# The last row block's normalisation: its middle 256 columns scaled by ScalarE and offset by GpSimd, and its factor computed ahead of most centring

## The chip, the cores and the metric

The kernel runs on one core of a Trainium2 chip. The metric is the time of one execution on the device in microseconds (us). A core has TensorE (matrix products, PE in the profile), VectorE (DVE), ScalarE (ACT), GpSimd (POOL) and SyncE (SP, which here only issues DMAs), each with an instruction queue that it works off in order. They share an on-chip memory, SBUF; TensorE writes its results to a second one, PSUM.

## The reference

One decoder layer over 512 tokens of width 1024: two attention branches, an output projection, a layer norm, then a gated MLP with a causal convolution, and a second layer norm. All of it is float32. What matters here is the very last step, the second layer norm:

```python
ffn_out = (silu(h_gate) * h_val) @ w_down
x = layer_norm(alpha * x + (1 + gt2) * ffn_out, ln2_g, ln2_b)

def layer_norm(x, g, b):
    mu = mean(x, axis=-1); var = mean((x - mu) ** 2, axis=-1)
    return (x - mu) * rsqrt(var + 1e-5) * g + b
```

Mean and variance are taken along the 1024 columns of each row, so a row's normalisation can start only when its last column has been summed.

## The kernel before, in words

The 512 rows are handled as four blocks of 128 rows (the 128 partitions of SBUF); a block's 1024 columns lie in two tiles of 512, `r[i][0]` and `r[i][1]`. Every float32 product is done as three products of split operands. The down projection is a Strassen-like scheme of sums of quarter blocks; blocks 0 and 1 are finished and stored earlier, and the end of the kernel belongs to blocks 2 and 3.

In the last loop (L1345 to L1358), `i` is 0 for block 2 and 1 for block 3. TensorE computes the last products of that block's second half. For block 2 that is one piece of 512 columns; for block 3 there are two pieces of 256 columns, so that VectorE can work on the first while TensorE still computes the second. The first piece's product is added to the residual in SBUF (L1356). For the second piece TensorE adds the residual itself (L1350, with the identity and the split residual `rest`), so its sum stays in PSUM. For each piece `V.bn_stats` (L1357) gathers the row statistics; those of the first 512 columns have been gathered earlier (L1329).

`ln_stats` (L899) turns the statistics into the mean `mu` and the normalising factor `rs`: VectorE merges them (L901), ScalarE takes a square root (L903), VectorE adds epsilon to the variance (L904), takes the reciprocal of the root (L905) and refines it by a Newton step (L906, L907). All of these work on one column. The factor comes out as -2 times the wanted one; the row of gains `lnr[0]` was multiplied by -0.5 beforehand to make up for it.

`tail` (L1239) then finishes a block on VectorE, piece by piece: centring (L1245) computes (x - mu) * gain, and scaling (L1249) computes x * rs + offset, with the offset row `lnr[1]`. Both are one instruction with three operands, two of them tiles. After each scaling, SyncE issues the store of that piece (L1250). For block 3 the pieces are columns 0 to 511, 512 to 767 (the middle one) and 768 to 1023 (read from PSUM).

Order: SyncE's queue is kept in program order. On the other engines a scheduler orders instructions by program order as priority and by when it holds their operands to be ready; so it puts the centrings between the steps of `ln_stats`. `tc.issue_after(ins)` adds an edge that keeps the block's instructions behind `ins` on the same engine, with no wait of its own.

Of the kernel before, what the change touches and what calls it, by code (L numbers as in the profile page):

```python
# [11 lines left out]
AF = mybir.ActivationFunctionType  # L12
ALU = mybir.AluOpType
# [38 lines left out]
def layer_kernel(ctx: ExitStack, tc: tile.TileContext, out, xT, x, c8, wa0, wa1, bcol, w1, wct, wv, bf,  # L52
# [3 lines left out]
    V, S, G, PE = nc.vector, nc.scalar, nc.gpsimd, nc.tensor  # L56
# [14 lines left out]
    cnt, state = [0], {"load": 0, "proc": 0}  # L71

    def nm(s):
        cnt[0] += 1
        return f"{s}_{cnt[0]}"

    def bank():
        return pp.tile([P, 512], F32, name=nm("ps"), tag="ps")
# [41 lines left out]
    s = V.tensor_tensor(sel, s3, ident[:, 64:72], ALU.add)  # L120
    def top_half(ap):
        return ap.bitcast(BF16).rearrange("p (c t) -> p c t", t=2)[:, :, 1]

    ctop = top_half(crow)
    with tc.issue_after(s.ins):
        s = V.tensor_tensor(crow[32:40], c8s, top_half(c8s), ALU.subtract)
# [21 lines left out]
    def z(dt, s, shape=(P, 512)):  # L148
        return zp.tile(list(shape), dt, name=nm(s), tag="z", bufs=NZ)
# [748 lines left out]

    def ln_stats(st):  # L899
        mv = cons.tile([P, 8], F32, name=nm("mv"), tag="mv", bufs=2)  # L900
        V.bn_aggr(mv[:, 0:2], st)  # L901
        v, s, y, t = mv[:, 2:3], mv[:, 3:4], mv[:, 4:5], mv[:, 5:6]
        S.activation(s, mv[:, 1:2], AF.Sqrt, bias=epsc)  # L903
        V.tensor_scalar_add(v, mv[:, 1:2], EPS)  # L904
        V.reciprocal(y, s)  # L905
        V.scalar_tensor_tensor(t, y, y, v, ALU.mult, ALU.mult)  # L906
        V.scalar_tensor_tensor(y, t, -3.0, y, ALU.add, ALU.mult)  # L907
        return mv[:, 0:1], y

    def ln_row(n):  # L910
# [14 lines left out]
    lnr = []  # L925
# [17 lines left out]
    def o_norm(i):  # L943
        xn, ps2 = o_st.pop(i)
        st = cons.tile([P, 2, 6], F32, name=nm("st"), tag="st", bufs=2)
        for e in range(2):
            ps = ps2[e]
            V.scalar_tensor_tensor(xn[e], xn[e], ALPHA, ps, ALU.mult, ALU.add)
            V.bn_stats(st[:, e, :], xn[e])
        mu, rs = ln_stats(st)  # L950
        for e in range(2):
            V.tensor_scalar(xn[e], xn[e], mu, rs, ALU.subtract, ALU.mult)
        x1.append(xn)
# [83 lines left out]
    for n in range(2 * FT):  # L1037
# [7 lines left out]
        if n in (23, 27):  # L1045
            t = t13[(23, 27).index(n)][:, 0:512]
# [124 lines left out]
    for n in range(2 * FT):  # L1171
        if n < NSPLIT:
            h, l = items[wui[n]][4]
            ps = bks[n]
            up_mm(ps, h, l, slice(256, 512))
        else:
            ps = bank()
# [21 lines left out]
        t = z(F32, "cv")  # L1199
# [6 lines left out]
        if n % 2 == 1:  # L1206
            g, v = hc
# [31 lines left out]
    def tail(i, st, pieces, eng, src):  # L1239
        tb = slice(i * P, (i + 1) * P)  # L1240
        mu, rs = ln_stats(st[:, 0 : len(pieces), :])
        for (e, c0, c1), ps in zip(pieces, src):
            c = slice(e * 512 + c0, e * 512 + c1)
            v = r[i][e][:, c0:c1]
            V.scalar_tensor_tensor(v, v if ps is None else ps, mu, lnr[0][:, c], ALU.subtract, ALU.mult)  # L1245
        for e, c0, c1 in pieces:
            c = slice(e * 512 + c0, e * 512 + c1)
            v = r[i][e][:, c0:c1]
            V.scalar_tensor_tensor(v, v, rs, lnr[1][:, c], ALU.mult, ALU.add)  # L1249
            eng.dma_start(out[tb, c], v)  # L1250

    p1, u2, q1, u3, tm = [[fine(n) for _ in range(2)] for n in ("p1", "u2", "q1", "u3", "tm")]
# [45 lines left out]
    def first_rows(i):  # L1298
        st = stat_tile()
        for e in range(2):  # L1300
            V.bn_stats(st[:, e, :], r[i][e])
        tb = slice(i * P, (i + 1) * P)
        mu, rs = ln_stats(st[:, 0:2, :])
        for e in range(2):
            c, v = slice(e * 512, (e + 1) * 512), r[i][e]
            V.scalar_tensor_tensor(v, v, mu, lnr[0][:, c], ALU.subtract, ALU.mult)
            S.activation(v, v, AF.Copy, scale=rs)
            G.dma_start(out[tb, c], v, accum_op=ALU.add)
# [8 lines left out]
    lnr = lnr2  # L1317
# [13 lines left out]
    for n, k in enumerate(wi):  # L1331
        w = weights(k)
        for a, p in enumerate(range(2 * n, min(FP - LATE, 2 * n + 2))):
            t = ops[p][3]
# [4 lines left out]
    s = V.tensor_tensor(r[3][1], r[3][1], W1[1], ALU.add)  # L1339
# [5 lines left out]
    for i in range(2):  # L1345
        pieces = [(1, 0, 512)] if i == 0 else [(1, 0, 256), (1, 256, 512)]
        for n, (e, c0, c1) in enumerate(pieces):
            ps = bank()[:, 0 : c1 - c0] if i else W1[0]
            for m in range(2 * n):
                PE.matmul(ps, idr, rest[:, m * 256 : m * 256 + 256], start=m == 0, stop=False)  # L1350
            for q in range(LATE):
                t = ops[FP - LATE + q][3]
                product(ps, t[:, top[i]], t[:, bot[i]], wc[q][0][:, c0:c1], wc[q][1][:, c0:c1], i == 1 and n == 0 and q == 0, q == LATE - 1, i == 0)
            v = r[2 + i][e][:, c0:c1]
            if n == 0:
                V.tensor_tensor(v, v, ps, ALU.add)  # L1356
            V.bn_stats(sts[i][:, n + 1, :], ps if n else v)  # L1357
        tail(2 + i, sts[i], [(0, 0, 512)] + pieces, nc.sync, [None, None, ps] if i else [None] * 2)  # L1358
# [69 lines left out]
```

## Time and profile before

| | |
|---|---|
| median of 3 runs | 735.04 us (734.61 to 735.48) |
| the profiled execution | 734.07 us, its span 732.3 us |
| TensorE's granted clock | 0.997 |
| busy over the span: TensorE / VectorE / ScalarE / GpSimd | 722.5 / 601.1 / 391.7 / 88.0 us |

The profile's times count from the start of the span. Its lines name engine, source line, operation, output and inputs, shapes (partitions x elements) and types. A line with x2 or x3 merges neighbouring instructions; its duration runs from the first start to the last end. In square brackets stands how long the engine had been idle before, and what released it. In the rows of stages, after the length, come the busy time of TensorE, its weight loads, VectorE, ScalarE and GpSimd with the number of instructions, then the granted clock, the DMA engines' busy share and GB/s. In the groups of instructions the figures after the bar are the total busy time, the mean in ns, and the idle time ahead.

### The profile page before, as it was taken

Reading aid. Unit: us, or ns where it says so; the run is one execution under the profiler, and the core shown is the slowest. Engines: PE = TensorE matmul, PEld = TensorE weight load, DVE = VectorE, ACT = ScalarE, POOL = GpSimd, SP = SyncE. Lnnn points to the kernel's source line nnn. Section 1 sums busy time; section 2 is a strip of 40 time slices with the busy share of each in tenths; the row PEclk is TensorE's granted clock in tenths of the full one; section 3 lists DMA queues with packets and bytes.
Section 4 is the critical chain, followed back from the end, with each engine's and each line's share of the span. In section 5 each row is a group of like instructions: output and inputs, shape, how many; then the busy total and the mean of one; then the engine's idle time right before and its main releaser. Section 6 shows DMA issues by size and latency. Waiting matters only on the chain.

```text
span 732.3 us, 9843 instructions
## 1 busy us (share of the span) xinstructions
PE 722.5 (99%) x3444; PEld 602.5 (82%) x3444; DVE 601.1 (82%) x1041; ACT 391.7 (53%) x684; POOL 88.0 (12%) x142
## 2 busy tenths in 40 slices
PE   8999999999999999999999999999999999999995
PEld 5878888888888888888889888888888888888885
DVE  7978799778898886883687999978887887679996
ACT  5576466686885754442056553454453544347550
POOL 1045224352010000000000001000011010000010
PEclk9999999999999999999999999999999999999998
DMA  9953435323332241632075688587698777657734
GB/s 358 404 207 126 173 116 197 148 88 115 118 116 99 75 171 59 224 128 86 1 259 139 216 248 238 169 252 227 189 359 245 217 238 209 200 164 224 219 91 93
DMA packets 45202, 131.96 MB, mean 180 GB/s; under 512 B 6136, under 2 KB 6656, under 8 KB 45152
## 3 DMA queue, kind: packets, MB, share of 16 engines
q1 hardware_dynamic: 37888, 112.61, 44.6%
q0 software_dynamic: 4224, 10.30, 7.4%
q10 hardware_dynamic: 3040, 8.42, 3.1%
q8 instruction: 27, 0.44, 0.2%
q14 instruction: 23, 0.19, 0.1%
HBM read 118.39 MB, written 12.85 MB: 179 GB/s over the span
## 4 chain that ended last, share of the span: by engine, by line
PE 97%; DVE 1%; DMA 0%; ACT 0%; issue 0%; DVEq 0%
PE ps L152 19%; PE ps L154 19%; PE ps L153 19%; PE ps L1148 5%; PE ps L1149 5%; PE ps L1150 5%; PE ps L369 5%; PE ps L613 3%; PE ps L595 2%; PE ps L521 2%; PE ps L523 2%; PE ps L522 2%; PE ps L939 2%; PE ps L941 2%; PE ps L940 2%; PE ps L547 1%
## 5 line engine op out<-in xcount | busy, mean ns | idle before, releaser
L217 ACT ACTIVATE wh<-raw 128x1024 fp32r<-128x1024 f32 (+1 forms) x105 | 109.0, 1040 | 106.5 <-PE ps L153 43.2
L94 DVE TENSOR_TENSOR wl<-raw,wh 128x1024 fp32r<-128x1024 f32 (+2 forms) x114 | 137.3, 1205 | 32.4 <-ACT wh L217 31.6
L152 PE MATMUL ps<-u2h,wh 128*128 128x512 f32 (+1 forms) x376 | 141.5, 376 | 0.0
L153 PE MATMUL ps<-u2l,wh 128*128 128x512 f32 (+1 forms) x376 | 141.3, 376 | 0.0
L154 PE MATMUL ps<-u2h,wl 128*128 128x512 f32 (+1 forms) x376 | 141.3, 376 | 0.0
L154 PEld LDWEIGHTS ps<-u2h,wl 128*128 128x128 f32 x376 | 70.8, 188 | 12.9
L152 PEld LDWEIGHTS ps<-u2h,wh 128*128 128x128 f32 x376 | 70.8, 188 | 12.7
L153 PEld LDWEIGHTS ps<-u2l,wh 128*128 128x128 f32 x376 | 70.8, 188 | 12.6
L152 PE MATMUL ps<-uh,wh 128*128 128x512 f32 x200 | 79.6, 398 | 0.0
L154 PE MATMUL ps<-uh,wl 128*128 128x512 f32 x200 | 78.2, 391 | 0.0
L153 PE MATMUL ps<-ul,wh 128*128 128x512 f32 x200 | 78.0, 390 | 0.0
L1201 ACT ACTIVATE cv<-ps,cw 128x512 f32<-128x512 f32 x44 | 34.0, 773 | 42.4 <-PE ps L154 36.0
L1202 DVE SCALAR_TENSOR_TENSOR cv<-ps,cw,cv 128x511 f32<-128x511 f32 x44 | 32.8, 746 | 21.6 <-ACT cv L1201 21.5
L154 PEld LDWEIGHTS ps<-uh,wl 128*128 128x128 f32 x200 | 37.6, 188 | 8.4
L153 PEld LDWEIGHTS ps<-ul,wh 128*128 128x128 f32 x200 | 37.7, 188 | 7.4
L152 PEld LDWEIGHTS ps<-uh,wh 128*128 128x128 f32 x200 | 37.6, 188 | 7.3
L240 DVE SCALAR_TENSOR_TENSOR raw<-raw,cbc 128x1024 f32<-128x1024 f32 x32 | 39.6, 1240 | 0.0
L575 POOL TENSOR_TENSOR pt<-pt,om 128x127 f32<-128x127 f32 (+3 forms) x32 | 38.6, 1217 | 1.3 <-DVE om L574 1.3
L181 POOL DMA_DIRECT2D raw<-in_wdp x10 | 8.9, 889 | 243.8 <-DMA raw<-in_wdp 227.7
L1203 DVE SCALAR_TENSOR_TENSOR cv<-ps,cw,cv 128x510 f32<-128x510 f32 x44 | 32.7, 744 | 0.4
L1209 ACT ACTIVATE cv<-cv 128x512 f32<-128x512 f32 x22 | 13.9, 631 | 34.1 <-DVE cv L1203 34.1
L574 DVE TENSOR_TENSOR_SCAN om<-om,dg 128x127 f32<-128x127 f32 (+3 forms) x32 | 28.8, 960 | 3.9 <-ACT om L569 3.9
(245 smaller groups left out, 1551.0 us busy)
## 6 DMA issues: line engine op xcount, KB each, us to landing
raw<-in_wup SPq DMA_DIRECT2D x44, 512.0 KB, 5.0
raw<-in_wa SPq DMA_DIRECT2D x32, 512.0 KB, 3.7
raw<-in_wct SPq DMA_DIRECT2D x25, 512.0 KB, 4.5
raw<-in_wdp SPq DMA_DIRECT2D x20, 512.0 KB, 5.3
wa<-in_wa SPq DMA_DIRECT2D x16, 512.0 KB, 8.7
raw<-in_wdp SPq DMA_DIRECT2D x22, 256.0 KB, 4.9
raw<-t SPq DMA_DIRECT2D x22, 256.0 KB, 4.3
raw<-in_wdp POOLq DMA_DIRECT2D x10, 512.0 KB, 7.7
```

The source lines that it names most:

```text
L94: state["read"] = V.tensor_tensor(o, i, fl(hi), ALU.subtract)
L152: PE.matmul(ps, wh, ah, start=first, stop=False)
L153: PE.matmul(ps, wh, al, start=False, stop=False)
L154: return PE.matmul(ps, wl, ah, start=False, stop=last)
L217: state["hi"] = S.activation(h[:, 0:cols], r[:, 0:cols], AF.Copy)
L240: state["read"] = V.scalar_tensor_tensor(wt[:, c], wt[:, c], 1.0, cbc[:, c] if by is None else by, ALU.mult, ALU.mult, accum_out=o)
L369: m = PE.matmul(grp[g], w, u, start=j == 0 and n == 0, stop=j == KT - 1 and n == 2)
L575: G.tensor_tensor(pt[b][:, s : e - 1], pt[b][:, s : e - 1], om[:, s + 1 : e], ALU.mult)
L1148: PE.matmul(ps, ah, bh, start=first, stop=False, skip_group_check=onto)
L1149: PE.matmul(ps, ah, bl, start=False, stop=False, skip_group_check=onto)
L1150: return PE.matmul(ps, al, bh, start=False, stop=last, skip_group_check=onto)
L1201: S.activation(t, ps, AF.Identity, bias=cw[:, n, 3:4], scale=cw[:, n, 2:3])
```

## The change

For block 3 alone (`late`, three pieces) the pieces are taken in the order middle, first, last. The middle piece is centred first, held only behind the merge of the statistics (L901); the centring of the other two is held behind the last step of the factor (L907). The middle piece's scaling by `rs` is an activation on ScalarE, its offset an addition on GpSimd; the other two keep VectorE's single instruction. The stores follow in the new order, all three on SyncE as before. For block 2 the order and the engines stay, and its centrings get an edge to L901, whose result they read in any case.

```diff
@@ ln_stats
-        V.bn_aggr(mv[:, 0:2], st)
+        state["mu"] = V.bn_aggr(mv[:, 0:2], st)
...
-        V.scalar_tensor_tensor(y, t, -3.0, y, ALU.add, ALU.mult)
+        state["rs"] = V.scalar_tensor_tensor(y, t, -3.0, y, ALU.add, ALU.mult)
@@ tail
-        for (e, c0, c1), ps in zip(pieces, src):
+        late = len(pieces) == 3
+        order = [1, 0, 2] if late else range(len(pieces))
+        for n in order:
+            (e, c0, c1), ps = pieces[n], src[n]
             c = slice(e * 512 + c0, e * 512 + c1)
             v = r[i][e][:, c0:c1]
-            V.scalar_tensor_tensor(v, v if ps is None else ps, mu, lnr[0][:, c], ALU.subtract, ALU.mult)
-        for e, c0, c1 in pieces:
+            with tc.issue_after((state["rs"] if late and n != 1 else state["mu"]).ins):
+                s = V.scalar_tensor_tensor(v, v if ps is None else ps, mu, lnr[0][:, c], ALU.subtract, ALU.mult)
+        for n in order:
+            e, c0, c1 = pieces[n]
             c = slice(e * 512 + c0, e * 512 + c1)
             v = r[i][e][:, c0:c1]
-            V.scalar_tensor_tensor(v, v, rs, lnr[1][:, c], ALU.mult, ALU.add)
+            if late and n == 1:
+                S.activation(v, v, AF.Copy, scale=rs)
+                G.tensor_tensor(v, v, lnr[1][:, c], ALU.add)
+            else:
+                V.scalar_tensor_tensor(v, v, rs, lnr[1][:, c], ALU.mult, ALU.add)
             eng.dma_start(out[tb, c], v)
```

## The prediction

> **What bounds the kernel now.** I read the profile from the outside in: first the chain of work that ended last, then the busy times by stage, then the timeline of the last stage, and last the DMA queue behind it.
>
> ```profile
> PE 97%; DVE 1%; DMA 0%; ACT 0%; issue 0%; DVEq 0%
> ```
>
> ```profile
> 724.96:732.30 7.34, 0.00 (x0) 0.00 (x0) 4.07 (x12) 0.29 (x1) 0.00 (x0) 0.74 0.35 129
> ```
>
> The kernel is TensorE's until 724.96 us; the change touches nothing before that. What follows lasts 7.34 us, 1.0% of the span, with TensorE and GpSimd idle and ScalarE busy 0.29 us. So all that the change can win or lose lies in a stage whose VectorE work is 4.07 us. A difference of 0.2% of the median, 1.47 us, is about what a measurement of this kernel can tell from no change.
>
> ```profile
> 724.96 0.43 DVE L1357 BATCH_NORM_STATS2 st<-ps 128x6 f32<-128x256 f32 x1 [0.52 <-PE ps L1150]
> 725.43 0.24 DVE L901 BATCH_NORM_AGGREGATE mv<-st 128x2 f32<-128x18 f32 x1
> 725.70 0.15 DVE L904 TENSOR_SCALAR mv<-mv 128x1 f32<-128x1 f32 x1
> 725.76 0.29 ACT L903 ACTIVATE mv<-mv,epsc 128x1 f32<-128x1 f32 x1 [4.74 <-DVE mv L901]
> 725.77 0.74 DVE L1245 SCALAR_TENSOR_TENSOR xn<-xn,mv,ln 128x512 f32<-128x512 f32 x1
> 726.43 0.16 DVE L905 RECIPROCAL mv<-mv 128x1 f32<-128x1 f32 x1
> 726.50 0.47 DVE L1245 SCALAR_TENSOR_TENSOR xn<-xn,mv,ln 128x256 f32<-128x256 f32 x1
> 726.88 0.21 DVE L906 SCALAR_TENSOR_TENSOR mv<-mv 128x1 f32<-128x1 f32 x1
> 727.01 0.48 DVE L1245 SCALAR_TENSOR_TENSOR xn<-ps,mv,ln 128x256 f32<-128x256 f32 x1
> 727.41 0.15 DVE L907 SCALAR_TENSOR_TENSOR mv<-mv 128x1 f32<-128x1 f32 x1
> 727.59 1.54 DVE L1249 SCALAR_TENSOR_TENSOR xn<-xn,mv,ln 128x512 f32<-128x512 f32 x3
> ```
>
> Columns: start, duration, engine, line. VectorE runs without a gap: the three centrings (L1245) fill the waits inside the normalising factor (L905 to L907), and three scalings (L1249) follow. A row's duration overlaps the next start, so I price by spacing: 0.66 us for the 512-wide centring (725.77 to 726.43), 0.38 for the middle one, 0.40 for the one that reads PSUM.
>
> ```profile
> 728.26 0.88 DVE L1249 SCALAR_TENSOR_TENSOR xn<-xn,mv,ln 128x256 f32<-128x256 f32 x2
> ```
> ```profile
> 728.66 0.48 DVE L1249 SCALAR_TENSOR_TENSOR xn<-xn,mv,ln 128x256 f32<-128x256 f32 x1
> ```
> ```profile
> 728.37 0.33 SPq L1250 DMA_DIRECT2D out<-xn  x1
> ```
> ```profile
> 728.81 0.86 SPq L1250 DMA_DIRECT2D out<-xn  x2
> ```
> ```profile
> 729.28 0.39 SPq L1250 DMA_DIRECT2D out<-xn  x1
> ```
> ```profile
> DMA to landing us min/median/max: 2.0/2.0/2.1
> ```
> ```profile
> 729.10:729.30 0.20, 0.00 (x0) 0.00 (x0) 0.04 (x1) 0.00 (x0) 0.00 (x0) 0.50 0.44 174
> ```
>
> The scalings start at 727.59, 728.26 and 728.66 and the last ends at 729.14. SyncE issues the three stores, in program order, at 728.37, 728.81 and 729.28. The last issue is 0.14 us behind its scaling, because SyncE can only follow one store by the next after 0.44 and 0.47 us. Each store lands 2.0 to 2.1 us after its issue, whatever its size; by the row of busy shares (the last two figures are the DMA engines' share and GB/s) data begins to move at about 729.2, some 0.8 us behind the first issue. So the end is the last issue plus 2.0, plus about 1.0 of closing waits up to 732.3. The term to forecast is the time of that last issue.
>
> **The change, part by part.** For the last row block it runs the middle centring first, holds the other two behind L907, and gives the middle 256 columns' scaling to ScalarE and their offset to GpSimd, whose store now stands first on SyncE. For the row block before it, the order of pieces stays and the added edge repeats a data dependence, so I cost it at nothing; what covers it if VectorE's order shifts there all the same is the 0.52 us that VectorE idles for TensorE before 724.96.
>
> The front of the tail, up to the middle centring at 725.77, keeps its times. The square root ends at 726.05, and the centring's 0.38 us of spacing covers it, so L905 can start at 726.15. From there the three small instructions stand bare. Another place shows that price:
>
> ```profile
> 356.75 0.16 DVE L905 RECIPROCAL mv<-mv 128x1 f32<-128x1 f32 x1 [0.17 <-ACT mv L903]
> 356.95 0.22 DVE L906 SCALAR_TENSOR_TENSOR mv<-mv 128x1 f32<-128x1 f32 x1
> 357.20 0.16 DVE L907 SCALAR_TENSOR_TENSOR mv<-mv 128x1 f32<-128x1 f32 x1
> 357.40 1.00 DVE L952 TENSOR_SCALAR xn<-xn,mv 128x512 f32<-128x512 f32 x2
> ```
>
> That is 0.65 us from L905 to the next work, where before they cost 0.07 + 0.13 + 0.18 = 0.38 between the centrings. So the change pays 0.27 there and takes one scaling, 0.40, off VectorE: 0.13 won. The factor is ready at 726.15 + 0.45 + 0.16 = 726.76 instead of 727.56. The 512 centring starts at 726.80, the PSUM one at 727.46, the 512 scaling at 727.86, the last scaling at 728.53, ending at 729.01 against 729.14. With SyncE's spacing the last issue would be at about 729.12, 0.16 earlier. That is the sum on durations alone, and it has nothing for what ScalarE and GpSimd do.
>
> ```profile
> 711.74 0.15 DVE L907 SCALAR_TENSOR_TENSOR mv<-mv 128x1 f32<-128x1 f32 x1
> ```
> ```profile
> 709.90 0.28 ACT L903 ACTIVATE mv<-mv,epsc 128x1 f32<-128x1 f32 x1
> 711.92 1.34 ACT L1307 ACTIVATE xn<-xn,mv 128x512 f32<-128x512 f32 x2 [1.74 <-DVE mv L907]
> ```
> ```profile
> L559 ACT ACTIVATE pt<-pt,sm 128x512 f32<-128x512 f32 x8 | 5.7, 711 | 0.0
> L559 ACT ACTIVATE pt<-pt,sm 128x256 f32<-128x256 f32 x8 | 4.0, 496 | 0.8 <-DVE sm L558 0.8
> L1307 ACT ACTIVATE xn<-xn,mv 128x512 f32<-128x512 f32 x4 | 2.7, 712 | 1.7 <-DVE mv L907 1.7
> ```
>
> The same scaling by the factor runs at L1307, 0.03 us behind L907 and straight behind a square root, with no table load between them. It is 712 ns at 512 columns, like L559's 711, so I take L559's 496 ns for 256. Nothing else is queued on ScalarE. The scaled piece is ready at 726.76 + 0.03 + 0.50 = 727.29.
>
> ```profile
> 48.59 1.19 ACT L418 ACTIVATE fp<-ps 8x512 f32<-8x512 f32 x2
> 49.87 1.82 POOL L422 TENSOR_TENSOR fp<-fp,fp 8x512 f32<-8x512 f32 x1 [8.04 <-ACT fp L418]
> ```
> ```profile
> 166.32 0.64 POOL L575 TENSOR_TENSOR pt<-pt,om 128x255 f32<-128x255 f32 x1
> 167.50 1.10 POOL L575 TENSOR_TENSOR pt<-pt,om 128x511 f32<-128x511 f32 x1
> ```
> ```profile
> 167.58 2.11 DVE L94 TENSOR_TENSOR wl<-raw,wh 128x1024 fp32r<-128x1024 f32 x1 [0.20 <-ACT wh L217]
> ```
> ```profile
> L94 DVE TENSOR_TENSOR wl<-raw,wh 128x1024 fp32r<-128x1024 f32 x101 | 125.6, 1244 | 31.9 <-ACT wh L217 31.6
> ```
> ```profile
> 121.44 1.16 DVE L94 TENSOR_TENSOR pl<-ps,ph 128x512 fp32r<-128x512 f32 x2
> 121.90 1.08 POOL L575 TENSOR_TENSOR pt<-pt,om 128x511 f32<-128x511 f32 x1
> ```
> ```profile
> L575 POOL TENSOR_TENSOR pt<-pt,om x32: 437/1100/2356, 54.3 to 167.5; 128x127 f32<-128x127 f32 x8, 128x383 f32<-128x383 f32 x8, 128x255 f32<-128x255 f32 x8, 128x511 f32<-128x511 f32 x8
> ```
>
> GpSimd took up ScalarE's result 0.09 us after its end (49.78 to 49.87), so its add would be ready at 727.38. A 255-wide one took 0.64 us by itself; across all widths they took 0.44 to 2.36. I take 0.64, the row nearest in width, and keep 2.36 as the far end. The pair at 167.5 shows what an add does to VectorE: the add kept its 1.10 us, and L94, which reads two SBUF tiles and started 0.08 behind it, took 2.11 where its mean is 1.244. It was held 0.87 us, nearly what was left of the add. The pair at 121.9, with a VectorE source in PSUM, shows no hold: 1.16 for two, and 1.08 for the add. So the add contends with the 512 centring and with both scalings, but not with the PSUM centring.
>
> The Trainium skill (SBUF — State Buffer, section "Who interferes with whom") says it as a rule: a VectorE instruction with two SBUF inputs and a GpSimd instruction that reads SBUF exclude each other, and the later to issue waits for the whole of the earlier. By that rule the sum becomes the one below, +0.15; without it, it stays at −0.16; the trace agrees, with the 0.87 us above.
>
> The add, ready at 727.38, finds the 512 centring running until 726.80 + 0.74 = 727.54, and then runs beside the PSUM centring until 728.18. The 512 scaling, due at 727.86, is held to 728.18: 0.32 lost. The scalings then end at about 728.93 and 729.33. The middle store is issued at 728.21 and off SyncE in time; the 512 store follows at 728.96 and the last at 728.96 + 0.47 = 729.43, against 729.28. Sum: **+0.15 us**. The cover that hides the middle store is thin: as long as the add ends before about 728.45, it costs SyncE nothing; each microsecond beyond that delays both other stores by the same, since they stand behind it.
>
> The profiled execution took 734.07 us, 1.77 more than its span of 732.3; the three timed runs have a median of 735.04 (734.61 to 735.48), 0.97 above it. The change adds 0.15 to either: 734.2 for the profiled one, 735.2 for the median.
>
> Bounds of the unknown costs: the most to gain is a scaling at no price for the bare factor, 0.40; the most to lose by one add is the far end below.
>
> **Rivals.**
> *No hold.* If short scalings are not held, the sum on durations stands: −0.16, 734.9. For it: the add is 0.64 us and half of it lies beside the PSUM centring. Against it: the 0.87 us.
>
> *The add comes last.* If VectorE's scalings get the SBUF side first, the add waits for 729.01, ends at 729.65, and the stores go out at 729.68, 730.12 and 730.59: last issue 1.31 later, 736.35, slower. It decides once the add ends after 728.45. For it: any 0.5 us more on ScalarE or in the handoff puts the add behind the 512 scaling's start at 727.86. Against it: by the rows above the add is ready half a microsecond before. If it slips in between the two scalings instead (728.60 to 729.24), the stores go out at 729.27, 729.71 and 730.18: +0.9.
>
> *A long add.* With the longest of L575's rows, 2.36 from 727.38, it ends at 729.74 and the last store goes out at 729.77 + 0.44 + 0.47 = 730.68: +1.40, at the edge of 0.2%. Anything more is measurably slower.
>
> *The order isn't what the change says.* If VectorE still interleaves centrings with the factor, the factor comes at about 727.5, the add at 728.1 to 728.8 or later, and the result is near the +0.9.
>
> **How the numbers follow.** The forecast case, +0.05 to +0.3, 0.50. No hold, −0.4 to 0: 0.26. The add between or behind the scalings, or a kept order, +0.5 to +1.4: 0.18. A long add over 1.47 us: 0.04. A gain over 1.47 us, for which no row offers room: 0.02. Only the last two leave the 0.2%, so: faster 0.02, same 0.94, slower 0.04. The range takes in the no-hold case (734.9) less the runs' lower spread of 0.43, so 734.4, and reaches up to the case of the add last, 736.3.
>
> **What would show it.** In the changed profile: L905 to L907 in one row of about 0.65 us behind the middle centring; ScalarE's scaling near 726.8 for 0.50; GpSimd's add from about 727.5 for 0.64; the 512 scaling stretched by about 0.3; three stores in the order middle, first, last, the last issue 0.1 to 0.2 later than 729.28 relative to the stats at 724.96. Wrong would be: an unstretched scaling (then faster by 0.16), an add that ends after the last scaling, a table load on ScalarE, or any difference before 724.96.

## The result, and the profile after

The changed kernel takes 736.03 us (median of 17 runs, 735.76 to 737.12) where the kernel before, run beside it, takes 734.91 (17 runs). The ratio is 1.0017, with a 95% interval of 1.0011 to 1.0023: slower by 0.8 to 1.7 us. That is inside the forecast range and, by the 0.2% bound, no change, but it is a real loss, some eight times the 0.15 us that the prediction added up.

The timeline of the tail after, by engine (columns as before: start, duration, engine and line), with line numbers of the changed kernel, where L1249 is the centring, L1255 and L1256 the new scaling and offset, L1258 the old scaling and L1259 the store:

```profile
725.85 0.43 DVE L1366 BATCH_NORM_STATS2 st<-ps 128x6 f32<-128x256 f32 x1 [0.52 <-PE ps L1150]
...
726.65 0.47 DVE L1249 SCALAR_TENSOR_TENSOR xn<-xn,mv,ln 128x256 f32<-128x256 f32 x1
727.05 0.16 DVE L905 RECIPROCAL mv<-mv 128x1 f32<-128x1 f32 x1
727.24 0.22 DVE L906 SCALAR_TENSOR_TENSOR mv<-mv 128x1 f32<-128x1 f32 x1
727.50 0.16 DVE L907 SCALAR_TENSOR_TENSOR mv<-mv 128x1 f32<-128x1 f32 x1
727.57 0.74 DVE L1249 SCALAR_TENSOR_TENSOR xn<-xn,mv,ln 128x512 f32<-128x512 f32 x1
728.23 0.47 DVE L1249 SCALAR_TENSOR_TENSOR xn<-ps,mv,ln 128x256 f32<-128x256 f32 x1
728.63 1.31 DVE L1258 SCALAR_TENSOR_TENSOR xn<-xn,mv,ln 128x512 f32<-128x512 f32 x2
```
```profile
727.69 0.51 ACT L1255 ACTIVATE xn<-xn,mv 128x256 f32<-128x256 f32 x1 [0.75 <-DVE mv L907]
```
```profile
728.28 0.72 POOL L1256 TENSOR_TENSOR xn<-xn,ln 128x256 f32<-128x256 f32 x1 [12.73 <-ACT xn L1255]
```
```profile
730.01 0.40 SPq L1259 DMA_DIRECT2D out<-xn  x1
```

The last row of VectorE there merges two scalings. The first of them, of 512 columns, by itself, after and before:

```profile
728.63 0.92 DVE L1258 SCALAR_TENSOR_TENSOR xn<-xn,mv,ln 128x512 f32<-128x512 f32 x1
```
```profile
727.59 0.75 DVE L1249 SCALAR_TENSOR_TENSOR xn<-xn,mv,ln 128x512 f32<-128x512 f32 x1
```

The last statistics start at 725.85 here and at 724.96 before. Four experiments below (e2, e3, e5, e6), whose work on TensorE and VectorE up to that point is the kernel before's, start them at 725.25, 725.20, 726.21 and 725.3, so I read that difference as one execution's own and compare the tails, counted from this start to the end of the span: 7.34 us before, 734.5 − 725.85 = 8.65 after, 1.31 more. That covers the loss in the timed runs, 1.12 us between the medians. A tail is read from one profiled execution of each kernel.

Up to the last store nothing was lost. Its issue lies 730.01 − 725.85 = 4.16 us into the tail, and before it lay 729.28 − 724.96 = 4.32 into it: 0.16 earlier. The loss comes later, in the closing sequence, which the profile books on the line of the launch (L1424 before, L1433 after): each engine ends with a drain (DRAIN), and then the engines wait for each other at a barrier made of semaphores (EVENT_SEMAPHORE). First SyncE's own drain, which follows the landing of the last store, before and after (columns: count, then minimum/median/maximum duration in ns, then the first and the last start):

```profile
L1424 SPq DRAIN  x2: 7/7/7, 731.5 to 731.5; - x2
```
```profile
L1433 SPq DRAIN  x2: 7/7/7, 732.3 to 732.4; - x2
```

SyncE is through 6.5 us into the tail in both. Then GpSimd's drain, before and after, its semaphores at the barrier after, and the waits of SyncE at the closing barrier before and after (in total, times, longest):

```profile
L1424 POOLq DRAIN  x1: 8165/8165/8165, 713.5 to 713.5; - x1
```
```profile
L1433 POOLq DRAIN  x1: 5426/5426/5426, 728.2 to 728.2; - x1
```
```profile
L1433 POOLq EVENT_SEMAPHORE  x2: 17/17/17, 733.7 to 733.8; - x2
```
```profile
SPq L1424 <- PEq L1424: 0.7, 2, 0.5
```
```profile
SPq L1433 <- PEq L1433: 2.0, 2, 1.5
```

Before, GpSimd had nothing to do behind its accumulating stores; its drain ran from 713.5 to 721.7, ten microseconds before anybody asked for it. After, its last instruction is the add, and the drain ends at about 733.65, some 4.65 us behind the add's end at 729.00, while SyncE is ready at 732.4. GpSimd signals the barrier at 733.7, and SyncE's wait there grows from 0.7 to 2.0: the 1.3 us. The rows of waits name TensorE's sequencer (PEq) as what released SyncE, but TensorE, ScalarE and VectorE had drained long before, by their rows at 725.85, 728.2 and 730.0:

```profile
L1433 PEldq DRAIN  x1: 2345/2345/2345, 723.5 to 723.5; - x1
```
```profile
L1433 ACTq DRAIN  x1: 539/539/539, 727.7 to 727.7; - x1
```
```profile
L1433 DVEq DRAIN  x1: 1239/1239/1239, 728.8 to 728.8; - x1
```

Of the drains ahead of the barrier, GpSimd's is the only one that ends behind SyncE's. No view that leaves out semaphores and drains shows this: in the timeline the last 4 us look empty, and the chain ends on VectorE.

### The profile page after: what moved, and what is told of

It reads as the page before. It is cut to its first block, busy times and chain, and to the rows that moved or that the text cites. A ratio compares the mean times of both kernels' runs of the same rounds, so it can differ in the third digit from the quotient of the medians.

```text
span 734.5 us, 9843 instructions
## 1 busy us (share of the span) xinstructions
PE 722.5 (98%) x3444; PEld 602.4 (82%) x3444; DVE 600.8 (82%) x1040; ACT 392.1 (53%) x685; POOL 88.7 (12%) x143
## 3 DMA queue, kind: packets, MB, share of 16 engines
q0 software_dynamic: 4224, 10.30, 7.1%
## 4 chain that ended last, share of the span: by engine, by line
PE 97%; DMA 1%; DVE 0%; ACT 0%; issue 0%; DVEq 0%
PE ps L152 19%; PE ps L154 19%; PE ps L153 19%; PE ps L1148 5%; PE ps L1149 5%; PE ps L1150 5%; PE ps L369 5%; PE ps L613 3%; PE ps L595 2%; PE ps L521 2%; PE ps L523 2%; PE ps L522 2%; PE ps L939 2%; PE ps L940 2%; PE ps L941 2%; PE ps L547 1%
## 5 line engine op out<-in xcount | busy, mean ns | idle before, releaser
L181 POOL DMA_DIRECT2D raw<-in_wdp x10 | 8.9, 886 | 245.6 <-DMA raw<-in_wdp 229.0
```

## The experiments

**Take GpSimd out, keep the rest (e1).**

```diff
-                G.tensor_tensor(v, v, lnr[1][:, c], ALU.add)
+                V.tensor_tensor(v, v, lnr[1][:, c], ALU.add)
```

> The changed kernel with the middle piece's offset added by VectorE in place of GpSimd; ScalarE still scales it, and the order stays. GpSimd then has no instruction in the last 18 us. Theory (the closing wait for GpSimd's drain, which ran to 733.65 in the changed kernel, is the loss): the tail from the start of the last statistics to the end of the span falls from 8.65 us to about 7.4 to 7.5 (VectorE's extra add puts the last store some 0.2 us later than the changed kernel's), so the time is within 0.3 us of the kernel before. Rival (the loss comes from the new order, the handoff to ScalarE or the store order): the tail stays at 8.4 us or more and the time about 1.2 us above the kernel before.

Measured: tail 734.3 − 726.87 = 7.43 us; 734.87 us, ratio to the kernel before 1.0001 (0.9992 to 1.0010). GpSimd's drain is back at its old place:

```profile
L1433 POOLq DRAIN  x1: 8158/8158/8158, 715.5 to 715.5; - x1
```

So ScalarE, the new order, the early factor, the new store order and VectorE's extra add cost some 0.1 us together; the rest hangs on GpSimd's add.

**Add only a GpSimd instruction (e2, e3).** In the kernel before, with `rs` of the last row block (e2) or of the one ahead (e3, `== 2`):

```diff
             eng.dma_start(out[tb, c], v)
+        if len(pieces) == 3:
+            G.tensor_copy(const([P, 1], F32, "scr"), rs)
```

> The kernel before with one GpSimd copy of one column (the normalising factor of the last row block to a tile that nothing reads), ready some 2.6 us behind the last statistics' start; nothing waits for it and no store is behind it. It leaves the result as it is. Theory (GpSimd's drain ends some 4.7 us behind the end of its last instruction, and the closing barrier waits for it): the drain ends near 7.4 us behind the start of the last statistics, against 6.5 for the stores, so the tail grows from 7.34 to about 8.1 to 8.3 us, 0.8 to 1.0 slower. Rival (the port, the handoff or the store order is the loss): the copy is free, the tail stays at 7.3 to 7.4 us and the time at that of the kernel before.

> The kernel before with the same one-column GpSimd copy, but of the factor of the row block before the last, some 2.3 us ahead of the last statistics' start and 5 us earlier than in e2. Theory: the drain then ends about 2.5 to 3 us behind the last statistics' start, under the stores, so the tail stays at 7.3 to 7.4 us and nothing is lost. Rival (any GpSimd instruction behind the accumulating stores costs a fixed time at the close, whenever it runs): the tail is that of e2.

GpSimd's copy and drain, in e2 and then in e3:

```profile
727.91 0.19 POOL L1252 COPY scr<-mv 128x1 f32<-128x1 f32 x1 [12.96 <-DVE mv L907]
```
```profile
L1426 POOLq DRAIN  x1: 4871/4871/4871, 727.9 to 727.9; - x1
```
```profile
723.04 0.19 POOL L1252 COPY scr<-mv 128x1 f32<-128x1 f32 x1 [8.13 <-DVE mv L907]
```
```profile
L1426 POOLq DRAIN  x1: 4871/4871/4871, 723.0 to 723.0; - x1
```

e2: tail 733.6 − 725.25 = 8.35 us, 735.62 us, ratio 1.0009 (1.0000 to 1.0017). e3: tail 732.5 − 725.20 = 7.30, 734.32 us, 0.9994 (0.9985 to 1.0003). A copy of 0.19 us that nobody waits for costs 1 us in the tail if it runs 2.7 us behind the last statistics' start, and nothing 4.9 us earlier. The same drain follows in both; in e3 it ends at 727.9, under the stores. By its time alone e2 is barely clear of the kernel before (its interval begins at 1.0000; the medians differ by 0.8 us, the low end of what was expected); the reading rests on the tails.

**The order alone (e4).** The changed kernel with L1258's single instruction for the middle piece too.

```diff
-            if late and n == 1:
+            if False:
```

> The changed kernel with the middle piece scaled and offset by VectorE's single instruction as before: only the order and the early factor are left. Theory: no GpSimd drain, so the end is VectorE's chain: the three bare factor steps cost some 0.15 to 0.25 us more than before, so the tail is 7.5 to 7.6 us and the time 0.1 to 0.3 above the kernel before, which is hardly measurable. Rival (the new order is the loss): the tail is 8.4 us or more, the time 1.2 above.

Measured: tail 733.1 − 725.58 = 7.52 us; 734.93 us, ratio 1.0002 (0.9993 to 1.0011). As expected; the order with the bare factor costs 0.18 us by the tail. Against e1 (7.43), a scaling on ScalarE with an add on VectorE is 0.09 better, which one execution of each hardly shows.

**The same copy later, and a memset (e5, e6).** In the kernel before, e5 copies a column of the first scaled piece; e6 fills the helper column that L907 has read.

```diff
             eng.dma_start(out[tb, c], v)
+            if len(pieces) == 3 and c0 == 0 and e == 0:
+                G.tensor_copy(const([P, 1], F32, "scr"), v[:, 0:1])
```
```diff
+        state["t"] = t
         return mv[:, 0:1], y
...
             eng.dma_start(out[tb, c], v)
+        if len(pieces) == 3:
+            G.memset(state["t"], 0.0)
```

> The kernel before with the one-column GpSimd copy of e2, but of the first scaled piece, so that it runs some 0.8 us later, about 3.5 us behind the last statistics' start. Theory (GpSimd's drain ends 4.7 us behind the end of its last instruction, whatever else runs): e2's tail of 8.35 us grows by the same 0.8 to 9.1 or 9.2 us, and the time is some 1.7 us above the kernel before. Rival (a fixed cost at the close, or a drain that ends at a fixed time): the tail stays at 8.35.

> The kernel before with a GpSimd memset of one column in place of e2's copy: it fills the helper column that the last factor step has just read, so it runs at the same time, and it reads no tile. Theory (any GpSimd instruction is followed by the long drain): the tail is 8.2 to 8.4 us, as with the copy. Rival (only an instruction that reads SBUF, or whose code has not run for long, is followed by it): the tail stays at 7.3 to 7.4 us.

Their instruction and drain, e5 first:

```profile
729.66 0.38 POOL L1252 COPY scr<-xn 128x1 f32<-128x1 f32 x1 [13.75 <-DVE xn L1249]
```
```profile
L1426 POOLq DRAIN  x1: 5062/5062/5062, 729.6 to 729.6; - x1
```
```profile
727.96 0.10 POOL L1253 MEMSET mv<- 128x1 f32 x1 [12.95 <-DVE mv L907]
```
```profile
L1427 POOLq DRAIN  x1: 4781/4781/4781, 727.9 to 727.9; - x1
```

e5: tail 735.5 − 726.21 = 9.29 us, 736.60 us, ratio 1.0025 (1.0015 to 1.0035). The copy runs 0.79 us deeper in the tail than e2's and takes 0.19 longer; the tail grows by 0.94, a little more than expected because the copy took longer. e6: tail 733.5 − 725.3 = 8.2, 735.62 us, 1.0009 (0.9999 to 1.0019), by its time not clear of the kernel before. The drain's record begins about with the instruction; less the instruction's own time it is 4.871 − 0.19, 5.062 − 0.38, 4.781 − 0.10, each 4.68 us, and 5.426 − 0.72 = 4.71 for the changed kernel's add. (The drain's record begins 0.02 us ahead of the copies' and the memset's and 0.04 ahead of the add's, so in all of them the drain ends some 4.66 us behind the instruction.) What the instruction does makes no difference.

**What the length depends on (e7, e8, e11, e12).** Kernels that leave the whole layer out and store zeros; VectorE adds a tile to itself until all DMAs have long landed, then GpSimd copies one column. Each ran once. From e7 to e8, and what e11 has beside e7's stores (the comments are added here):

```diff
     for i in range(NB):
-        nc.sync.dma_start(out[i * P : (i + 1) * P, :], a)    # e7
+        G.dma_start(out[i * P : (i + 1) * P, :], a)          # e8
```
```diff
+    for i in range(16):                                      # e12: 4
+        G.dma_start(tc.dram_tile([P, 1 * 1024], F32, name=f"d{i}"), a)    # e12: 4 * 1024
```

> A kernel that leaves out the whole layer: it stores zeros to the output by SyncE, lets VectorE add a tile to itself 20 times (some 23 us) and then has GpSimd copy one column. No DMA is issued by GpSimd anywhere. If the long drain belongs to GpSimd's own close, GpSimd's drain ends 4.7 us behind the copy here too. If it is a wait for what GpSimd's DMAs left behind, the drain is short (0.1 us or so).

> The kernel of e7 with its four stores issued by GpSimd instead of SyncE, landed long before the copy. By the first reading the drain is 4.7 us, as in e7; by the second it is short in e7 and 4.7 us here.

> The kernel of e7 with 16 DMAs of 512 KB issued by GpSimd to memory that nothing reads (its output is zeros, stored by SyncE, and the layer is left out), and 40 adds on VectorE, so that all have landed long before the copy. By the number of DMAs the drain ends 0.09 + 16 x 0.085 = 1.4 to 1.5 us behind the copy; by bytes (four times e8's) 1.4 to 1.5 too.

> The kernel of e11 with the same bytes in 4 DMAs of 2 MB. By the number of DMAs the drain ends 0.4 to 0.5 us behind the copy, as in e8; by bytes or packets 1.4 to 1.5, as in e11.

The drains of e7, e8, e11 and e12 in this order, and the copy of e11 (it takes 0.18 in all four):

```profile
L132 POOLq DRAIN  x1: 271/271/271, 28.2 to 28.2; - x1
```
```profile
L132 POOLq DRAIN  x1: 614/614/614, 28.3 to 28.3; - x1
```
```profile
L134 POOLq DRAIN  x1: 1594/1594/1594, 53.4 to 53.4; - x1
```
```profile
L134 POOLq DRAIN  x1: 614/614/614, 56.7 to 56.7; - x1
```
```profile
53.47 0.18 POOL L68 COPY s<-b 128x1 f32<-128x1 f32 x1 [32.70 <-DVE b L67]
```

Less the copy: 0.09 us with no GpSimd DMA, 0.43 with four, 1.41 with sixteen, and 0.43 again with four that move the bytes of the sixteen. e7's short drain speaks for the second of its two readings, but the 4.7 us that e8 was to show by it did not come: four DMAs gave a tenth of that, and so the question became what the length goes with. It is not bytes; each DMA that GpSimd has issued adds some 0.083 us, although all had landed long before (in e11 the DMA engines are idle from about 30 us on, and the copy runs at 53.47). Packets are not told apart from DMAs here: GpSimd's queue carried 576 in e8, 2304 in e11 and 576 again in e12, so e12's expectation was wrong in putting packets with bytes. The full kernel separates them.

**The same in the full kernel (e9, e10).** By its groups the full kernel has 56 GpSimd DMAs: 12 at L181, 16 at L443 and L444, 12 at L652, 3 at L654, 5 at L1019, 4 at L1024 and 4 at the accumulating stores. 0.09 + 56 x 0.082 is 4.68. e9 is the changed kernel, and e10 the kernel before, with 28 of them moved:

```diff
-        G.dma_start(s2t[n][66:68, :], chi[h : h + 1, :, :])
-        G.dma_start(m2t[n][64:66, :], chi[h : h + 1, :, :])
+        S.dma_start(fl(s2t[n][66:68, :]), fl(chi[h : h + 1, :, :]))
+        S.dma_start(fl(m2t[n][64:66, :]), fl(chi[h : h + 1, :, :]))
...
-            eng.dma_start(row[:, b, :], t[32 * b : 32 * b + j1 - j0, :])
+            S.dma_start(row[:, b, :], t[32 * b : 32 * b + j1 - j0, :])
```

> The changed kernel with 28 of the 56 DMAs that GpSimd issues in a run (L443, L444, L652, all before 540 us) issued by ScalarE instead; the tail is the changed kernel's. Theory, from e7 (drain 0.09 us behind the copy with no GpSimd DMA), e8 (0.43 with four) and the full kernel (4.65 to 4.68 with 56), that the drain grows by some 0.083 us for each DMA that GpSimd has issued: it falls to about 2.4 us behind the add, ends about 5.6 us behind the last statistics' start, under the stores' 6.5, and the tail falls from 8.65 to 7.2 or 7.3. Rival (the length comes from the kernel's length, its last accumulating stores or anything else at its end): the drain stays at 4.65 and the tail at 8.6.

> The kernel before with the same 28 DMAs issued by ScalarE: the control for e9, since moving them may cost or win time in the middle of the kernel. Theory: the tail stays at 7.3 us, since the drain was hidden here, and e9's time lies 0 to 0.1 us below this one's. Rival: e9's time lies 1.2 us above this one's.

e9's add and drain, and the bytes and packets that GpSimd's queue still carries in it:

```profile
727.89 0.72 POOL L1256 TENSOR_TENSOR xn<-xn,ln 128x256 f32<-128x256 f32 x1 [12.73 <-ACT xn L1255]
```
```profile
L1433 POOLq DRAIN  x1: 3134/3134/3134, 727.8 to 727.8; - x1
```
```profile
q0 software_dynamic: 3328, 10.23, 7.1%
```

The drain less the add is 3.134 − 0.72 = 2.41 us; 0.09 + 28 x 0.083 gives 2.41. Bytes hardly changed (10.30 to 10.23 MB) and packets fell by a fifth (4224 to 3328), while the drain fell by half, as the number of DMAs did. So neither bytes nor packets set the length. The drain now ends some 5.5 us into the tail, under the stores. e9: tail 733.0 − 725.46 = 7.54 us, 734.95 us, ratio to the kernel before 0.9999 (0.9990 to 1.0008); e10: 732.8 − 725.23 = 7.57, 734.83 us, 0.9998 (0.9989 to 1.0007). My expectation of 7.2 to 7.3 for both tails missed by 0.25. It is not the stores: the last issue lies 4.31 us into the tail in e10 and 4.32 in the kernel before, and data stops moving at 5.8 in both. In its close SyncE works through a row of semaphore waits, some 0.06 us apart. From the wait that the last store releases up to the drain there are seven of them in e10, and three in the kernel before:

```profile
L1424 SPq EVENT_SEMAPHORE  x7: 27/28/28, 731.5 to 731.9; - x7
```
```profile
L1424 SPq EVENT_SEMAPHORE  x3: 28/28/28, 731.3 to 731.4; - x3
```

By the trace's semaphore numbers the last store of e9 and e10 uses another semaphore, one that SyncE waits for earlier in that row. So some 0.24 us in the tails of these two (four waits more) comes from that, and the two are to be compared with each other. Against its own control the change without its drain is 0.03 better by the tail and cannot be told from it by the time. So no version here beats the kernel before by anything that can be measured.

## Why the prediction was right or wrong, point by point

- *The change touches only the tail, and 0.2% is 1.47 us:* right as to the tail, where the loss of 1.31 us lies. But 0.2% was not the least that can be told from no change: with 17 runs of each the interval is 0.06% to either side, and 0.17% is clear of it.
- *The three bare factor steps cost 0.65 us to the next work:* 727.05 to 727.57, 0.52. The 512 centring is held behind L907 but does not use its result, so it starts 0.07 behind L907's start and not 0.20. Against the 0.38 before, the steps cost 0.14 more and not 0.27.
- *ScalarE 0.03 behind the factor for 0.50, handoff to GpSimd 0.09, add 0.64:* 0.03, 0.51, 0.08 and 0.72. No table load came.
- *The add holds the 512 scaling by 0.32:* wrong in size. The scaling started at 728.63 with 0.37 us of the add's record left, and took 0.92 where it took 0.75 before: held by 0.17. In e9, which has the same add, it takes 0.92 too, and in e1, with VectorE's add in its place, 0.74. The rule of the Trainium skill (SBUF — State Buffer, section "Who interferes with whom"), by which the later one waits for the whole of the earlier, gave 0.37 here; the measurement decides against that size. Whether the add had done its reading by then, I did not test.
- *The last issue comes 0.15 us later:* it came 0.16 earlier. That is the value of the rival without a hold, but by luck: there was a hold. The last scaling ended 0.09 earlier in the tail (the 0.40 taken off VectorE, less 0.14 for the bare steps and 0.17 for the hold), and the last issue followed it by 0.07 where it was 0.14 before. e9 and e10 bear out that without the drain the change is about even.
- *"So the end is the last issue plus 2.0, plus about 1.0 of closing waits up to 732.3":* this is the step that failed. I took the closing waits as a constant behind the stores. They are a barrier over all engines, and what each engine must finish first is part of it: after the change the span ended 4.5 us behind the last issue (730.01 to 734.5) where the prediction counted 3.0. GpSimd's share was in the trace before, as a drain of 8.17 us that began at 713.5, but hidden by ten microseconds, and I took no account of it. Its price for this change, 1.3 us, is the whole result. "Where you give an idle engine its first late instruction, ask what its close costs" was the missing question.
- *The rivals:* "a long add" came out at nearly the measured size, +1.40, for the wrong reason: the add took 0.72 us, and no store waited for it beyond its issue. No rival named the mechanism that decided, and none of the signs of being wrong would have shown it. That 736.03 lies inside the range is luck: its upper end, 736.3, was set by the add coming last, and the add ended at 729.00, before either of VectorE's scalings did. The chance of 0.94 for "within 0.2%" was well placed only because the tail is so short.

## What to carry to other kernels

In these runs an engine's last instruction was followed by its close, and the kernel ended with the slowest close, not with the last store. Before work is given to an idle engine near the end, read the drains in the closing sequence: on GpSimd, the last instruction should end before the last store's landing by the drain's length, 4.7 us in this kernel with its 56 GpSimd DMAs. The same work earlier is free (e3), and so is the same place with fewer GpSimd DMAs in the run (e9).

## What the runs showed of the hardware that I had not expected

GpSimd's closing drain behind a late compute instruction took 0.09 us in a run in which GpSimd had issued no DMA, 0.43 with 4, 1.41 with 16, 2.41 with 28 and 4.68 to 4.71 with 56: some 0.083 us for each DMA issued in the run, the same for 512 KB and 2 MB, and although in the small kernels all had landed long before. A memset, a copy and an add were followed by the same drain. Why finished DMAs cost time there stays open, as does the longer drain (8.17 us before, 6.7 in e10) where GpSimd's last instructions were the accumulating stores themselves.
